# The front of a one-layer hybrid decoder kernel: how x and the first weights are loaded, where ScalarE loads its table, and how the S5 parameters share GpSimd

## The chip, the cores and the metric

The kernel runs on 1 core of one Trainium2 chip. The metric is the device time of one execution in microseconds (us), here the median of 3 runs; lower is better. A profiled execution has a span, from its first to its last instruction, and a time of its own that is a little longer than the span.

## The reference

One layer of a decoder on 256 tokens of width 2048, all in float32. The RMS norm of x feeds one combined input projection, whose columns go to three token mixers (retention, mLSTM and S5). Their outputs are joined and projected back, added to x, and a gated convolutional feed-forward layer of inner width 5632 and a last norm follow.

```python
def reference(x, norm1_w, w_in, ...):
    h = rmsnorm(x, norm1_w[l])
    x = x + token_mixer(h, w_in[l], ...)      # retention, mLSTM, S5, then @ w_out
    h = rmsnorm(x, norm2_w[l])
    x = x + conv_ffn(h, ffn_w_up[l], ffn_conv_w[l], ffn_conv_b[l], ffn_w_down[l])
    return rmsnorm(x, final_norm_w)

def s5(u, a_re, a_im, log_step, b_re, b_im, ...):
    step = jnp.exp(log_step)[:, None]
    mag = jnp.exp(ar * step)
    abar_re, abar_im = mag * jnp.cos(ai * step), mag * jnp.sin(ai * step)
    xr, xi = abar_re - 1.0, abar_im
    den = ar * ar + ai * ai
    fr, fi = (xr * ar + xi * ai) / den, (xi * ar - xr * ai) / den
    bbar_re = fr[..., None] * br - fi[..., None] * bi
    ...
```

The S5 parameters (`step`, `mag`, cosine and sine, `fr`, `fi`, and powers of the rotation) depend on weights alone. The norm's factor 1/rms depends on x; the kernel multiplies it in behind the projection.

## The kernel before, in words

Every product is made of three: a weight item is loaded as float32 (`wr`), rounded by ScalarE to a shorter type (`wh`, line 193), and the rest is taken by VectorE (`wl = wr - wh`, line 183). TensorE multiplies both by the activations (line 234). Items are cut from one long stream in the order of use and numbered from 0. There are 4 buffers for `wr`, 4 for `wh` and 3 for `wl`. `loads_to`, `highs_to` and `lows_to` issue load, rounding and rest of the items up to a number.

The front is the projection to the S5 input u: items 0 to 3 of 512 columns (one k-tile of 128 rows each) and 4 to 9 of 1024 columns (two k-tiles each). Its loop runs over these 10 items, splits the k-tiles of x that belong to one into high and low part (`s`), and adds into four accumulators (two `acc`, one `u` of double size). In its later steps it also squares x for the norm. x comes in pieces, `load_x`, on the same queue (SP) as the weights. In the loop of before, step j issues the load of the x piece and the weight item of step j+4.

Behind the front come 6 tiles of 128 output rows (two items of 1024 columns each, from item 10 on), then tiles that are token-major. The norm's factor is taken as follows: TensorE sums the squares (`mis <- onesm,s`), VectorE scales the sum (`t <- mis`), GpSimd raises it to -1/2 (`t <- t,neg_half`), VectorE puts it on a diagonal (`s <- ident,t`), and TensorE spreads it over the partitions (`mis <- s,onesm`); the last stands in TensorE's program between two matmul groups of the 6 tiles.

The order in this half of the program is written by a planner while the kernel is built: side tasks are generators that yield the engine and the time from which they can go on, and `pump` resumes one when the estimated clock of that engine (`clk.dve`, `clk.pe`, ...) has come that far. Each engine then runs its own instructions strictly in that order. `s5_params` is such a task: some 125 small GpSimd instructions of 128x12 to 128x16, issued through `Pool` (line 217) and costed by it. In the kernel before, it yields once ahead of a reciprocal on VectorE and once behind all powers of the rotation, so all that GpSimd has to do for it stands in one row.

Of the kernel before, what the change touches and what calls it, by code (L numbers as in the profile page):

```python
# [10 lines left out]
F32 = mybir.dt.float32  # L11
# [29 lines left out]
def kernel(ctx: ExitStack, tc: tile.TileContext, a: dict, out: bass.AP):  # L41
# [162 lines left out]
    class Pool:  # L204

        @staticmethod
        def __getattr__(fn):
            real = getattr(nc.gpsimd, fn)

            def go(o, *args, **kw):  # L210
                n = free(o)
                if fn == "tensor_tensor":
                    c = 0.3 + 0.1645 * n if kw["op"] == ALU.pow else 0.148 + 0.0021 * n
                else:
                    c = 0.16 + 0.00083 * n
                run("pool", c, [o], args + tuple(kw.values()))
                return real(o, *args, **kw)  # L217
            return go
# [155 lines left out]
    def loads_to(i):  # L374
        while nxt[0] <= min(i, len(items) - 1):
            j = nxt[0]
            ap, n = items[j]
            t = reuse("wr", wraw.tile([128, CH], F32, tag="wr", name=f"wr{j}"), 4)
            for i, z in enumerate(ap):
                nc.sync.dma_start(out=t[:, i * n // len(ap):(i + 1) * n // len(ap)], in_=z)  # L380
            if not auto[0]:
                free_at = max([x[3] for x in was_read.get(t.tensor.name, ())], default=0.0)
                clk.dma = max(clk.dma, free_at + 1.3) + n / 703.0
                landed(t, clk.dma + 0.91)
            if later:

                dst, src = later.pop(0)
                nc.sync.dma_start(out=dst, in_=src)
                clk.dma += free(dst) / 703.0
                landed(dst, clk.dma + 0.91)  # L390
                loaded.add(dst.tensor.name)
            raw[j] = t
            nxt[0] += 1
# [36 lines left out]
    neg_half = const.tile([128, 12], F32, name="neg_half")  # L430

# [140 lines left out]

    def s5_params():
        sh = [128, 16]
        step_ = exp_(P("ls"), sh)
        arg, th = tn(sh), tn(sh)
# [10 lines left out]
        G.tensor_scalar(ph, ph, 0.125, None, op0=MUL)  # L587
        G.tensor_tensor(z, ph, ph, op=MUL)
        G.tensor_scalar(s, z, -1 / 5040, None, op0=MUL)
        G.tensor_scalar(v, z, 1 / 40320, None, op0=MUL)  # L590
        for cs, cc in ((1 / 120, -1 / 720), (-1 / 6, 1 / 24), (None, -0.5)):
            if cs is not None:
                G.scalar_tensor_tensor(s, s, cs, z, op0=ADD, op1=MUL)
            G.scalar_tensor_tensor(v, v, cc, z, op0=ADD, op1=MUL)
        G.scalar_tensor_tensor(s, s, 1.0, ph, op0=ADD, op1=MUL)
        G.tensor_scalar(v, v, 1.0, 1.0, op0=MUL, op1=ADD)
        mag = exp_(arg, sh)

# [8 lines left out]
        for _ in range(3):  # L607
            v, s = square(v, s)
        ar, ai = P("are"), P("aim")
# [7 lines left out]
        yield after(den)  # L617
        V.reciprocal(den, den)
        for o, x0, x1_, op in ((fr, xr_, xi_, ADD), (fi, xi_, xr_, SUB)):
            G.tensor_tensor(t1, x0, ar, op=MUL)  # L620
            G.tensor_tensor(t2, x1_, ai, op=MUL)
            G.tensor_tensor(o, t1, t2, op=op)
            G.tensor_tensor(o, o, den, op=MUL)
        turn = {1: (v, s)}
        for m in (1, 2, 4, 8, 16, 32, 64):
            turn[2 * m] = square(*turn[m])
        yield after(fi)
# [486 lines left out]
    nc.gpsimd.memset(onesm, 1.0)  # L1114
    nc.gpsimd.memset(neg_half, -0.5)
    clk.dma += 0.15

    warm = mis_t()
    for _ in range(11):
        mm(warm[:, :128], lhsT=onesm, rhs=onesm, start=True, stop=True)  # L1120
    clk.pe = 5.6
# [15 lines left out]
    for j in range(4):  # L1137
# [30 lines left out]
    clk.dve = 3.3  # L1168
    clk.act = 2.8
# [10 lines left out]
    for j, ks in enumerate(kts):  # L1180
# [13 lines left out]
        if j + 4 < NU:  # L1194
            load_x(kts[j + 4][0], len(kts[j + 4]))
# [8 lines left out]
        if j >= NU - 7 and len(sqs) < 8:  # L1204
            square()
# [354 lines left out]
```

## Time and profile before

| | |
|---|---|
| median of 3 runs | 1166.82 us (1166.51 to 1167.03) |
| profiled execution, its own time | 1166.34 us |
| its span | 1164.3 us |
| TensorE busy in the span | 1141.4 us, 98% |
| VectorE, ScalarE, GpSimd busy | 868.8, 625.9, 86.3 us |
| TensorE's granted clock, mean of the span | 0.992 |

TensorE is busy almost all the time; what it loses it loses in few places. "Busy" counts an instruction as long as it lasts, so at the lower of the two clocks TensorE is busy twice as long for the same work. The profiled execution lies 0.48 us under the median of the runs.

### The profile page before, as it was taken

Reading aid. Unit: us, or ns where it says so; the run is one execution under the profiler, and the core shown is the slowest. Engines: PE = TensorE matmul, PEld = TensorE weight load, DVE = VectorE, ACT = ScalarE, POOL = GpSimd, SP = SyncE. Lnnn points to the kernel's source line nnn. Section 1 sums busy time; section 2 is a strip of 40 time slices with the busy share of each in tenths; the row PEclk is TensorE's granted clock in tenths of the full one; section 3 lists DMA queues with packets and bytes.
Section 4 is the critical chain, followed back from the end, with each engine's and each line's share of the span. In section 5 each row is a group of like instructions: output and inputs, shape, how many; then the busy total and the mean of one; then the engine's idle time right before and its main releaser. Section 6 shows DMA issues by size and latency. Waiting matters only on the chain.

```text
span 1164.3 us, 18162 instructions
## 1 busy us (share of the span) xinstructions
PE 1141.4 (98%) x6742; PEld 1015.7 (87%) x6742; DVE 868.8 (75%) x1479; ACT 625.9 (54%) x982; POOL 86.3 (7%) x226
## 2 busy tenths in 40 slices
PE   8699999999999999999999999999999999999997
PEld 7589888999988888888888888888888888888897
DVE  7488999989968668778777778777787655544554
ACT  7275546456657556555555555555555544444441
POOL 7704311001000000000000000000000000000000
PEclk9899999999999999999999999999999999999998
DMA  8546745545657656565555656555566666666663
GB/s 291 164 138 185 238 134 154 163 136 163 188 186 239 201 181 189 186 190 187 190 189 187 192 185 193 185 189 191 185 192 187 184 184 193 186 190 186 194 193 106
DMA packets 66906, 215.21 MB, mean 185 GB/s; under 512 B 7553, under 2 KB 9601, under 8 KB 66817
## 3 DMA queue, kind: packets, MB, share of 16 engines
q1 hardware_dynamic: 66672, 214.01, 59.1%
q8 instruction: 52, 0.85, 0.3%
q14 instruction: 38, 0.30, 0.1%
q10 hardware_dynamic: 144, 0.04, 0.0%
HBM read 211.92 MB, written 2.10 MB: 184 GB/s over the span
## 4 chain that ended last, share of the span: by engine, by line
PE 91%; POOL 6%; issue 1%; DVE 1%; DMA 0%; POOLq 0%; ACT 0%; DVEq 0%
PE acc L234 87%; POOL tp L217 3%; PE mis L234 3%; POOL t L217 2%; PE wo L234 1%; DVE s L183 1%; PE mis L238 0%; DVE wl L183 0%; DMA pp<-in_pp_dram 0%; DVE t L183 0%; POOLq L1556 0%; ACT s L202 0%; DVE tp L183 0%; DVEq L1556 0%; PE pj L234 0%
## 5 line engine op out<-in xcount | busy, mean ns | idle before, releaser
L183 DVE TENSOR_TENSOR wl<-wr,wh 128x1024 fp32r<-128x1024 f32 (+3 forms) x415 | 480.7, 1160 | 240.4 <-PE acc L234 211.2
L193 ACT CAST wh<-wr 128x1024 fp32r<-128x1024 f32 (+3 forms) x415 | 413.0, 997 | 372.8 <-PE acc L234 330.7
L234 PE MATMUL acc<-s,wh 128*128 128x512 f32 x2372 | 604.1, 394 | 3.3 <-DVE s L183 3.3
L234 PEld LDWEIGHTS acc<-s,wh 128*128 128x128 f32 x2372 | 426.6, 189 | 81.1 <-DVE s L183 4.2
L234 PEld LDWEIGHTS acc<-s,wl 128*128 128x128 f32 x2372 | 327.5, 190 | 26.0 <-DVE wl L183 1.0
L234 PE MATMUL acc<-s,wl 128*128 128x256 f32 x2372 | 336.6, 282 | 0.5 <-DVE wl L183 0.5
L234 PE MATMUL acc<-wh,s 128*128 128x384 f32 (+2 forms) x632 | 158.4, 329 | 0.0
L183 DVE SCALAR_TENSOR_TENSOR s<-s,pp,s 128x255 f32<-128x255 f32 (+3 forms) x244 | 116.2, 479 | 5.7 <-ACT s L202 2.6
L183 DVE TENSOR_TENSOR s<-s,s 128x256 f32<-128x256 f32 (+5 forms) x242 | 111.5, 474 | 5.5 <-ACT s L193 2.8
L234 PEld LDWEIGHTS acc<-wh,s 128*128 128x128 f32 x632 | 112.2, 189 | 1.9 <-issue 1.2
L234 PE MATMUL acc<-wl,s 128*128 128x384 f32 (+2 forms) x316 | 103.1, 326 | 0.0
L202 ACT ACTIVATE s<-s,pp 128x256 f32<-128x256 f32 (+1 forms) x146 | 82.4, 568 | 24.2 <-DVE s L183 24.1
L217 POOL TENSOR_TENSOR t<-t,neg_half 128x2 f32<-128x2 f32 (+1 forms) x4 | 2.5, 633 | 882.1 <-DVE t L183 882.1
L202 ACT ACTIVATE s<-s 128x256 f32<-128x256 f32 (+2 forms) x106 | 45.6, 431 | 33.3 <-DVE s L183 33.1
L183 DVE TENSOR_TENSOR s<-acc,s 128x256 f32<-128x256 f32 x138 | 57.4, 417 | 4.4 <-PE acc L234 3.2
L234 PEld LDWEIGHTS acc<-wl,s 128*128 128x128 f32 x316 | 59.6, 189 | 0.0
L193 ACT COPY s<-acc 128x256 f32<-128x256 f32 x136 | 49.3, 364 | 12.5 <-PE acc L234 12.5
L234 PE MATMUL acc<-g,wh 128*128 128x512 f32 x196 | 50.0, 394 | 0.0
L183 DVE TENSOR_TENSOR s<-s,rbc 128x256 f32<-128x256 f32 x106 | 44.5, 424 | 4.2 <-ACT rbc L193 1.3
L234 PEld LDWEIGHTS acc<-g,wh 128*128 128x128 f32 x196 | 34.8, 188 | 6.2
L234 PE MATMUL mis<-s,s 128*32 128x256 f32 (+6 forms) x280 | 29.4, 352 | 0.0
L234 PEld LDWEIGHTS acc<-g,wl 128*128 128x128 f32 x196 | 27.1, 189 | 2.3
(106 smaller groups left out, 467.5 us busy)
## 6 DMA issues: line engine op xcount, KB each, us to landing
wr<-in_wup_dram SPq DMA_DIRECT2D x176, 512.0 KB, 4.7
wr<-in_wdn_dram SPq DMA_DIRECT2D x70, 512.0 KB, 3.8
wr<-in_wtm_dram SPq DMA_DIRECT2D x56, 384.0 KB, 3.4
wr<-in_wfm_dram SPq DMA_DIRECT2D x36, 512.0 KB, 4.5
wr<-in_wout_dram SPq DMA_DIRECT2D x26, 512.0 KB, 4.6
wr<-in_wdt_dram SPq DMA_DIRECT2D x11, 512.0 KB, 3.8
s<-in_x_dram SPq DMA_DIRECT2D x14, 256.0 KB, 5.4
wr<-in_wdn_dram SPq DMA_DIRECT2D x14, 256.0 KB, 2.7
```

The costliest lines, as they stand in the source:

```text
L183: return real(o, *args, **kw)
L193: return nc.scalar.copy(o, i)
L202: return nc.scalar.activation(o, i, fn, **kw)
L217: return real(o, *args, **kw)
L234: nc.tensor.matmul(o, lhsT=lhsT, rhs=rhs, start=start, stop=stop)
```

## The change

Five things. All x pieces and all 10 items of the front are loaded ahead of the loop; items 4 to 9 go into six of the eight `s4` buffers, which the S5 groups use later on, in place of `wr` buffers. A small ScalarE activation of one column stands at the very start of ScalarE's program, and the table load ahead of it. The S5 task yields after each few instructions until the planner's VectorE clock reaches its GpSimd clock (`keep_up`), and the planner's cost of a small GpSimd instruction is raised to some 0.4 us. The reciprocal of `den` becomes a power of -1 on GpSimd. And 9 instead of 11 warm-up matmuls, one square fewer ahead of its time, and other start values of the planner's clocks.

```diff
-                    c = 0.3 + 0.1645 * n if kw["op"] == ALU.pow else 0.148 + 0.0021 * n
+                    c = 0.3 + 0.1645 * n if kw["op"] == ALU.pow else 0.4 + 0.0021 * n
                 else:
-                    c = 0.16 + 0.00083 * n
+                    c = 0.4 + 0.00083 * n
...
-            t = reuse("wr", wraw.tile([128, CH], F32, tag="wr", name=f"wr{j}"), 4)
+            if NS <= j < NU:
+
+                t = s4()
+            else:
+                t = reuse("wr", wraw.tile([128, CH], F32, tag="wr", name=f"wr{j}"), 4)
...
+    neg_one = const.tile([128, 16], F32, name="neg_one")
...
+    def keep_up():
+
+        return "dve", clk.pool
+
     def s5_params():
         sh = [128, 16]
         step_ = exp_(P("ls"), sh)
+        yield keep_up()
...
         mag = exp_(arg, sh)
+        yield keep_up()
...
         for _ in range(3):
             v, s = square(v, s)
+            yield keep_up()
...
-        yield after(den)
-        V.reciprocal(den, den)
+        G.tensor_tensor(den, den, neg_one, op=ALU.pow)
+        yield keep_up()
...
         for m in (1, 2, 4, 8, 16, 32, 64):
             turn[2 * m] = square(*turn[m])
-        yield after(fi)
+            yield keep_up()
...
+    nc.scalar.activation(tn([128, 1]), onesm[:, 0:1], AF.Square)
...
-    for _ in range(11):
+    for _ in range(9):
...
-    for j in range(4):
+    for j in range(NU):
         load_x(kts[j][0], len(kts[j]))
         loads_to(j)
...
-        if j + 4 < NU:
-            load_x(kts[j + 4][0], len(kts[j + 4]))
         loads_to(j + 4)
...
-        if j >= NU - 7 and len(sqs) < 8:
+        if j >= NU - 6 and len(sqs) < 8:
             square()
```

On GpSimd, the power for the norm's factor (`t <- t,neg_half`) stood behind the last power of the rotation:

```order
L217 TENSOR_TENSOR tp_660<-t_654 128x16
L217 TENSOR_SCALAR tp_664<-t_654 128x16
L217 TENSOR_TENSOR t_662<-tp_664,t_653 128x16
L217 TENSOR_SCALAR t_661<-tp_660 128x16
L217 TENSOR_TENSOR t_708<-t_597,neg_half 128x2
L664 MEMSET s_177_950 128x16
```

In the changed kernel it stands behind the second exponential (`mag`, the row `t_559`) and ahead of the first square of the rotation:

```order
L218 TENSOR_TENSOR tp_528<-tp_556,tp_527 128x16
L218 TENSOR_SCALAR tp_560<-tp_528 128x16
L218 TENSOR_TENSOR t_559<-tp_560,tp_529 128x16
L218 TENSOR_TENSOR t_632<-t_480,neg_half 128x2
L218 TENSOR_TENSOR tp_684<-t_488 128x16
L218 TENSOR_SCALAR tp_688<-t_488 128x16
```

It has moved ahead of 54 instructions of the S5 task; one more memset and the power of -1 have come in elsewhere in the row.

On VectorE, the stretch from the last sums of the front to the norm's diagonal (`s <- ident,t`) held two `wl` items with four products of the S5 matrices between them, and the reciprocal stood three rows ahead of its first row:

```order
L183 TENSOR_TENSOR s_146_678<-u_123,s_145_676 128x256
L183 TENSOR_TENSOR s_148_682<-u_123,s_147_680 128x256
L183 TENSOR_SCALAR t_597<-mis_598 128x2
L183 TENSOR_TENSOR wl_690<-wr_538,wh_570 128x1024
L183 TENSOR_TENSOR s_150_710<-s_95_441,t_274 128x512
L183 TENSOR_TENSOR s_152_712<-s_96_442,t_275 128x512
L183 TENSOR_TENSOR wl_722<-wr_561,wh_688 128x1024
L183 TENSOR_TENSOR s_151_711<-s_96_442,t_274 128x512
L183 TENSOR_TENSOR s_153_713<-s_95_441,t_275 128x512
L183 TENSOR_TENSOR s_156_744<-acc_560,s_155_742 128x256
L183 TENSOR_TENSOR wl_751<-wr_685,wh_720 128x1024
L183 TENSOR_SCALAR s_157_769<-ident,t_708 128x128 x2
```

In the changed kernel the same stretch reads (`wl_584` is item 13, `wl_666` item 16):

```order
L183 TENSOR_TENSOR s_105_573<-u_149,s_104_571 128x256
L183 TENSOR_TENSOR s_107_577<-u_149,s_106_575 128x256
L183 TENSOR_TENSOR wl_584<-wr_418,wh_450 128x1024
L183 TENSOR_TENSOR wl_613<-wr_441,wh_582 128x1024
L183 TENSOR_SCALAR t_480<-mis_602 128x2
L183 TENSOR_TENSOR s_112_636<-acc_440,s_111_634 128x256
L183 TENSOR_TENSOR wl_643<-wr_579,wh_611 128x1024
L183 TENSOR_TENSOR wl_666<-wr_608,wh_641 128x1024
L183 TENSOR_SCALAR s_118_692<-ident,t_632 128x128 x2
L183 TENSOR_TENSOR s_120_698<-acc_607,s_119_696 128x256
```

The reciprocal and the S5 products are gone from here (the products now stand some 45 rows further on, behind the `wl` of item 27), and one more item has its `wl` ahead of the diagonal: up to item 16, before up to item 15. On TensorE the spreading of the factor stands behind the five items 10 to 14, before behind the four items 10 to 13.

On the SP queue the order of the loads is the same, but the weight loads from item 4 on (`wr_293`, now `s_6_125`) waited for VectorE, which had to free a `wr` buffer:

```order
L1130 DMA s_76_291<-in_x_dram 128x512 [waits DMAHW1_49]
L380 DMA wr_293<-in_wu_dram 128x1024 [waits DMAHW2_49,DVE_49]
L1130 DMA s_78_310<-in_x_dram 128x512 [waits DMAHW3_49]
L380 DMA wr_312<-in_wu_dram 128x1024 [waits DMAHW4_49,DVE_49]
L1130 DMA s_80_329<-in_x_dram 128x512 [waits DMAHW5_49]
```

Now they wait for an earlier transfer alone:

```order
L1150 DMA s_5_123<-in_x_dram 128x512 [waits DMAHW1_49]
L385 DMA s_6_125<-in_wu_dram 128x1024 [waits DMAHW2_49]
L1150 DMA s_7_127<-in_x_dram 128x512 [waits DMAHW3_49]
L385 DMA s_8_129<-in_wu_dram 128x1024 [waits DMAHW4_49]
L1150 DMA s_9_131<-in_x_dram 128x512 [waits DMAHW5_49]
```

What has gone is the wait for VectorE; the wait for the transfer that used the same semaphore some 8 transfers earlier stays.

## Rows read from the trace of the kernel before

**Rows 1.** The page, part on the engines: busy us, share of the span, instructions

```profile
PE 1141.4 (98%) x6742; PEld 1015.7 (87%) x6742; DVE 868.8 (75%) x1479; ACT 625.9 (54%) x982; POOL 86.3 (7%) x226
```

**Rows 2.** Waits of TensorE, whole span: us in total, times, longest

```profile
PE mis L234 <- DVE s L183: 9.5, 2, 9.2
...
PE mis L238 <- POOL t L217: 1.2, 1, 1.2
```

**Rows 3.** Stretches: busy of PE, PEld, DVE, ACT, POOL; granted clock, DMA share, GB/s

```profile
9.00:10.00 1.00, 0.34 (x2) 0.30 (x3) 1.00 (x3) 1.00 (x3) 0.83 (x3) 1.00 1.14 313
14.00:15.00 1.00, 0.16 (x1) 0.16 (x2) 1.00 (x3) 1.00 (x2) 0.85 (x3) 0.99 1.05 418
15.00:16.00 1.00, 1.00 (x3) 0.81 (x4) 1.00 (x3) 1.00 (x3) 0.85 (x3) 0.50 1.01 404
18.00:19.00 1.00, 1.00 (x6) 0.81 (x5) 1.00 (x2) 1.00 (x4) 0.91 (x2) 0.80 0.99 381
55.00:56.00 1.00, 0.41 (x1) 0.41 (x2) 0.94 (x3) 0.00 (x0) 0.15 (x3) 0.50 0.00 0
59.00:60.00 1.00, 1.00 (x6) 0.82 (x6) 1.00 (x5) 1.00 (x2) 0.00 (x0) 0.82 0.00 0
```

**Rows 4.** TensorE in order of time: start, us, instruction, [idle before]

```profile
5.64 0.70 PE L234 MATMUL acc<-s,wh 128*128 128x512 f32 x2 [0.17 <-DVE s L183]
...
9.66 0.73 PE L234 MATMUL acc<-s,wh 128*128 128x512 f32 x2 [0.99 <-DVE s L183]
...
14.84 1.12 PE L234 MATMUL acc<-s,wh 128*128 128x512 f32 x2 [2.13 <-DVE s L183]
...
33.30 2.02 PE L234 MATMUL acc<-s,wh 128*128 128x512 f32 x8
...
45.14 1.21 PE L234 MATMUL acc<-s,wl 128*128 128x256 f32 x8 [0.55 <-DVE wl L183]
55.59 1.22 PE L234 MATMUL mis<-s,onesm 128*128 128x256 f32 x2 [9.24 <-DVE s L183]
```

**Rows 5.** VectorE in order of time, from 41 us on

```profile
41.82 0.25 DVE L183 RECIPROCAL t<-t 128x16 f32<-128x16 f32 x1 [6.41 <-POOL t L217]
...
55.05 0.48 DVE L183 TENSOR_SCALAR s<-ident,t 128x128 f32<-128x128 f32 x2 [4.91 <-POOL t L217]
```

**Rows 6.** GpSimd in order of time

```profile
13.33 1.13 POOL L217 TENSOR_SCALAR tp<-t 128x16 f32<-128x16 f32 x1
...
28.08 0.61 POOL L217 TENSOR_SCALAR tp<-t 128x16 f32<-128x16 f32 x1
...
37.95 0.22 POOL L217 TENSOR_TENSOR t<-tp,tp 128x16 f32<-128x16 f32 x1
...
54.29 0.73 POOL L217 TENSOR_TENSOR t<-t,neg_half 128x2 f32<-128x2 f32 x1
```

**Rows 7.** ScalarE in order of time, first 13 us

```profile
3.18 1.28 ACT L202 ACT_TABLE_LOAD   x1 [3.18 <-DMA s<-in_x_dram]
4.47 0.51 ACT L202 ACTIVATE s<-s,pp 128x256 fp32r<-128x256 f32 x1
...
12.09 1.05 ACT L193 CAST wh<-wr 128x1024 fp32r<-128x1024 f32 x1 [1.66 <-DMA wr<-in_wu_dram]
```

**Rows 8.** SP queue in order of time: issue of item 4

```profile
4.47 0.43 SPq L1130 DMA_DIRECT2D s<-in_x_dram  x1
6.24 0.33 SPq L380 DMA_DIRECT2D wr<-in_wu_dram  x1
```

**Rows 9.** The powers on GpSimd by form: busy us, mean ns

```profile
L217 POOL TENSOR_TENSOR t<-tp,neg_half 128x12 f32<-128x12 f32 x2 | 5.4, 2679 | 0.2
L217 POOL TENSOR_TENSOR t<-t,neg_half 128x2 f32<-128x2 f32 x2 | 1.4, 714 | 153.7 <-DVE t L183 153.7
```

**Rows 10.** VectorE in the front: `wl` of two steps that follow each other

```profile
15.71 1.24 DVE L183 TENSOR_TENSOR wl<-wr,wh 128x1024 fp32r<-128x1024 f32 x1
...
18.27 1.23 DVE L183 TENSOR_TENSOR wl<-wr,wh 128x1024 fp32r<-128x1024 f32 x1
```

More of the change, by code (lines that the diff above doesn't have):

```diff
@@ L608, in s5_params @@
             v, s = square(v, s)
+            yield keep_up()
         ar, ai = P("are"), P("aim")
@@ L616, in s5_params @@
         G.tensor_scalar(xr_, xr_, 1.0, -1.0, op0=MUL, op1=ADD)
-        yield after(den)
-        V.reciprocal(den, den)
+        G.tensor_tensor(den, den, neg_one, op=ALU.pow)
+        yield keep_up()
         for o, x0, x1_, op in ((fr, xr_, xi_, ADD), (fi, xi_, xr_, SUB)):
@@ L623, in s5_params @@
             G.tensor_tensor(o, o, den, op=MUL)
+            yield keep_up()
         turn = {1: (v, s)}
@@ L626, in s5_params @@
             turn[2 * m] = square(*turn[m])
-        yield after(fi)
+            yield keep_up()
         yield "obj", lambda: "raws" in st
@@ L1114 @@
     nc.gpsimd.memset(onesm, 1.0)
+    nc.scalar.activation(tn([128, 1]), onesm[:, 0:1], AF.Square)
     nc.gpsimd.memset(neg_half, -0.5)
+    nc.gpsimd.memset(neg_one, -1.0)
     clk.dma += 0.15
     warm = mis_t()
-    for _ in range(11):
+    for _ in range(9):
         mm(warm[:, :128], lhsT=onesm, rhs=onesm, start=True, stop=True)
-    clk.pe = 5.6
+    clk.pe = 4.8
     xr, xat = [None] * 8, {}
@@ L1167 @@
     ups += [pair[:, :512], pair[:, 512:]]
-    clk.dve = 3.3
-    clk.act = 2.8
+    clk.dve = clk.pool = 3.3
+    clk.act = 2.6
     sqs = []
```

## The prediction

> **What bounds the kernel now.** I read the page first: TensorE is busy 1141.4 of 1164.3 us [rows 1], so the kernel is bound by TensorE, and a change can only win what TensorE loses by waiting or by running at the lower clock. Then I read who TensorE waits for [rows 2]: one wait of 9.2 us on VectorE is far ahead of the others. Third, TensorE in order of time [rows 4] shows that nearly all that is lost lies in the first 60 us, and fourth, the clock of short stretches [rows 3] shows what each long wait costs afterwards.
>
> There are two losses. The first is in the front. TensorE starts on it at 5.64, waits 0.99 us ahead of 9.66 and 2.13 us ahead of 14.84, and is through at 33.30 [rows 4]. Right after the second wait the granted clock is 0.50 (1.2 GHz); it is back at 2.4 GHz in 18 to 19, whose mean is 0.80, so at 18.40 [rows 3]. That is 3.4 us at half speed from 14.98 on: 1.7 us lost. The remaining 12 k-tiles therefore cost (33.30 - 14.84 - 1.7) / 12 = 1.40 us each.
>
> The second is the wait for the norm's factor. The matmul that spreads it starts at 55.59 after 9.24 us of idling, and 0.55 us were lost ahead of 45.14 [rows 4]. VectorE idles 4.91 us for GpSimd ahead of the diagonal, and 6.41 us ahead of the reciprocal [rows 5]; GpSimd comes to the norm's power only at 54.29, for 0.73 us [rows 6]. So the wait is GpSimd's: the power stands behind the whole S5 task. When TensorE goes on at 55.59 the clock is 0.50, until 59.36 (mean 0.82 in 59 to 60) [rows 3]: 1.9 us more. Sum of the second loss: 9.24 + 0.55 + 1.9 = 11.7 us.
>
> **The change, part by part.** The sum is made against the profiled execution's own time, 1166.34 us, which is 0.48 us under the median of the runs.
>
> *The table load.* It takes 1.28 us from 3.18 on, behind x's first piece, and the first ACTIVATE follows at 4.47 [rows 7]. Moved ahead of the data it lies beside the transfer, and TensorE can start some 1.0 us earlier, also since two warm-up matmuls are gone. I count nothing: k-tile 2 is not there earlier, so the wait ahead of 9.66 only grows from 0.99 to about 2 us.
>
> *The loads of the front.* Item 4 was issued at 6.24, although the queue was free at 4.90 [rows 8], and landed at 12.09, where ScalarE had waited 1.66 us for it [rows 7]; from there it took 2.75 us of rounding, rest and split until 14.84 [rows 4]. Without the wait for a buffer it can be issued 1.3 us earlier. It lands 1.3 us earlier if the transfers ahead of it leave room, and not at all earlier if they do not. The transfer rate was 313 GB/s in 9 to 10 and 404 to 418 later on [rows 3], so there was some room; I take 0.9 us, keep 0 and 1.3. The later items are no issue: one step of the loop takes VectorE 18.27 - 15.71 = 2.56 us [rows 10], TensorE 2 x 1.40 = 2.80. As to the clock: the wait ahead of item 4 shrinks from 2.13 us to some 1.3, but the one ahead of 9.66 grows. After 0.99 us the clock did not fall, after 2.13 it did; I give an even chance, half of 1.7 us. Front: 0.9 + 0.8 = 1.7 us won (bounds 0 and 1.3 + 1.7 = 3.0), so its end comes at 31.6.
>
> The Trainium skill ("DMA: Bandwidth & Descriptors", section Specifications) gives some 358 GB/s as what HBM yields to one core. The rows go to 418 GB/s, so this trace does not agree. By an estimate from the page's figure the 313 of 9 to 10 would be seven eighths of what is to be had, item 4 would come 0.3 us earlier at most, and the sum below would end 0.6 us later.
>
> *The norm's power ahead of 54 S5 instructions.* When does GpSimd reach it now? Ahead of it are the same instructions up to the end of the second exponential. Before, 46 of them took from 13.33 to 38.17 [rows 6], 0.54 us each; in the stretch where VectorE was always busy, 13.33 to 28.08, the 23 took 0.64 us each. VectorE will be busier now, as it no longer idles for the reciprocal, so I take 0.64 throughout: 13.33 + 46 x 0.64 = 42.8, and 43.5 with the power. At the other rate it would be 38.9. When is it wanted? TensorE took 46.35 - 33.30 - 0.55 = 12.5 us from the front's end through four items (10 to 13) and the sum of squares, some 3.0 us an item. Now five items stand ahead: 31.6 + 15.5 = 47.1. From diagonal to matmul it is 55.59 - 55.05 = 0.54 us, so the factor is wanted by 46.6. It is there 3 us earlier (3.1 to 7.7). VectorE comes to the diagonal when item 16 has its `wl`, that is when item 13 has left its buffer at 44.1, plus 1.23 us: 45.3, in time too.
>
> So the 9.24, the 0.55 and the 1.9 us at half speed all go: 11.7 us. What is late next is the work behind the factor: some 12 products of 128x256 on VectorE, 5 us, stand ahead of the `wl` of item 18, which would be ready at about 54. TensorE wants it three items and the high half of a fourth after 47.6, at 58. That is covered by 4 us.
>
> *The reciprocal as a power.* On VectorE it took 0.25 us, and VectorE stood 6.41 us for it [rows 5]; that idling is inside the 11.7. On GpSimd the power of 128x12 takes 2.68 us and of 128x2 0.71 [rows 9], 0.197 us an element, so 128x16 is 3.5 us by my estimate (no less than 2.68). It is hidden: its result goes into the S5 products, which now stand behind the `wl` of item 27. GpSimd has 27 instructions between the two powers and that result, at 0.64 us 17.3 us, and the power's 3.5: 43.5 + 20.8 = 64.3. Item 27's `wl` waits until item 24 is through, seven items of 3 us and three of 2.2 after 47.6, some 74 us. Cover 10 us. Without cover it would cost VectorE 3.5 us and TensorE as much.
>
> *The rest.* The 1.2 us wait for the gates' GpSimd chain [rows 2] may go, since that task's place is now planned with dearer instructions; the S5 products and groups come later against TensorE and may make new small waits. I put this at 0, with -1.2 and +3 as bounds.
>
> Sum: 1.7 + 11.7 + 0 = 13.4 us; 1166.34 - 13.4 = **1152.9 us**.
>
> **The rivals.**
>
> *The factor is still late.* GpSimd runs one instruction while VectorE runs one: 13.33 took 1.13 us beside a `wl` of 1.23, where others take 0.22 [rows 6, 10]. If VectorE, now with hardly a pause, held it to about 0.9 us an instruction, the power would come at 13.33 + 46 x 0.9 + 0.7 = 55.4, TensorE would wait 9 us with the half clock behind it, and only the 1.7 us of the front and the changed place of one item (3.0 us) would remain: some 1161. Half of that delay gives 1157. Against it: no stretch of [rows 6] is slower than 0.64 over many instructions. The Trainium skill ("GPSIMD Engine Reference", section 8, Key points) says that GpSimd shares its SBUF interfaces with VectorE and contends with instructions that have two SBUF inputs. The 1.13 us agree with it, and nearly all VectorE work of the front is of that kind.
>
> *A later wait gives it back.* VectorE's S5 work is put off behind item 27, so it is denser between 70 and 360 us. If the S5 groups end late, TensorE stands ahead of the output projection, and 4 to 8 us of the win are lost, with the half clock: 1157 to 1161. Against it: VectorE idled 6.41 and 4.91 us for GpSimd alone [rows 5], 11.3 of the 13.4 us that are taken away, so it loses hardly any time in which it worked.
>
> *Slower.* Should GpSimd's power of -1 and its 27 instructions end behind 74 us, VectorE stands at the S5 products, and behind them stand the `wl` of items 28 on; three `wl` buffers are 6 us, and then TensorE stands too, at half speed afterwards. The kernel is slower once this wait is over 13.4 us and 2.3 (0.2%), that is if GpSimd comes at about 96 us instead of 64. Price then: 1169 or more. It would need over 1.8 us an instruction.
>
> *The early loads do nothing.* Item 4 lands no earlier and the clock falls as before: 1154.6. That is inside the forecast's range.
>
> **How the numbers follow.** Forecast with its bounds: win 8.5 to 15.9 us (0 and 3.0 for the front, 11.7, -3 and +1.2 for the rest, none at its worst together), chance 0.74. Factor late, 1157 to 1161: 0.11. Later wait, 1157 to 1161: 0.09. Slower: 0.03. No effect that shows, if two of these meet: 0.03. The range 1150.5 to 1158.5 takes the forecast and the milder half of the two rivals beside it, and leaves some 2 in 10 out. 0.2% (2.3 us) is about what a measurement of this kernel can tell from no change; faster by more than that 0.94, within it 0.03, slower 0.03.
>
> **What would show it right or wrong.** Right: no wait over 1 us on TensorE between the front's end and 100 us; the power of 128x2 on GpSimd at 39 to 44 us, and VectorE's diagonal waiting for TensorE's buffers and not for GpSimd; the clock at 2.4 GHz from 35 to 60 us; the front's end at 30.3 to 33.3; the power of 128x16 some 3.5 us long; no VectorE wait at the S5 products. Wrong: a wait of VectorE for GpSimd ahead of the diagonal of more than 3 us, the front's end unchanged with its waits moved ahead, or TensorE waits over 2 us in total between 100 and 430 us.

## The result and the profile after

The changed kernel takes 1158.63 us (median of 4 runs, 1158.35 to 1159.89), the kernel before 1166.66 beside it (4 runs). The ratio is 0.9936, 95% interval 0.9924 to 0.9947: 8.0 us faster, where 13.4 were forecast, and just above the forecast range. The profiled execution has 1158.52 us and a span of 1156.5 (before 1164.3).

The page, part on the engines, and TensorE's waits over the whole span, as [rows 1, 2] of before:

```profile
PE 1140.5 (99%) x6738; PEld 1013.0 (88%) x6738; DVE 870.0 (75%) x1478; ACT 625.0 (54%) x983; POOL 95.0 (8%) x228
```

```profile
PE acc L235 <- DVE s L183: 4.3, 5, 1.5
PE mis L235 <- POOL t L218: 1.9, 1, 1.9
PE mis L235 <- DVE s L183: 1.9, 4, 1.0
PE mis L239 <- DVE s L183: 1.2, 1, 1.2
...
```

The wait of 9.2 us is gone. (The 1.9 us for GpSimd's `t` is in the tail of both kernels.) Yet TensorE is busy 1140.5 us, hardly less than the 1141.4 before, although the half-speed stretches are gone too: matmuls that wait in the middle of a group count as busy. In the rows further on, 28 matmuls of the last S5 group are busy 3.29 us, where all 32 take 1.93 in the kernel before.

**The first 60 us** went as forecast. The same places as [rows 4], in TensorE's order of time:

```profile
4.85 1.20 PE L235 MATMUL acc<-s,wh 128*128 128x512 f32 x2
...
9.50 0.73 PE L235 MATMUL acc<-s,wh 128*128 128x512 f32 x2 [0.99 <-DVE s L183]
...
14.04 0.73 PE L235 MATMUL acc<-s,wh 128*128 128x512 f32 x2 [1.50 <-DVE s L183]
...
30.95 2.00 PE L235 MATMUL acc<-s,wh 128*128 128x512 f32 x8
...
45.81 0.59 PE L235 MATMUL mis<-s,onesm 128*128 128x256 f32 x2
...
49.04 2.00 PE L235 MATMUL acc<-s,wh 128*128 128x512 f32 x8
```

The front ends 2.35 us sooner (30.95, before 33.30), the factor's matmul waits for nothing, and item 16 starts at 49.04. In the kernel before, item 16 is this row:

```profile
63.46 2.00 PE L234 MATMUL acc<-s,wh 128*128 128x512 f32 x8
```

TensorE is **14.4 us ahead** here. The clock did not fall: the granted clock in stretches of [rows 3] reads 1.00 (2.4 GHz) after the second wait and behind the factor.

```profile
15.00:16.00 1.00, 1.00 (x8) 0.87 (x8) 1.00 (x2) 1.00 (x3) 0.92 (x2) 1.00 1.01 393
55.00:56.00 1.00, 1.00 (x6) 0.80 (x5) 1.00 (x1) 0.88 (x2) 1.00 (x2) 1.00 0.80 171
```

GpSimd in order of time has the norm's power at 39.85 (before 54.29, [rows 6]) and the new power of 128x16; VectorE's diagonal, second fence, follows a `wl` that waited for TensorE's buffers and does not wait for GpSimd any more [rows 5]:

```profile
39.85 0.73 POOL L218 TENSOR_TENSOR t<-t,neg_half 128x2 f32<-128x2 f32 x1
...
47.70 3.09 POOL L218 TENSOR_TENSOR t<-t,neg_one 128x16 f32<-128x16 f32 x1
```

```profile
43.28 1.23 DVE L183 TENSOR_TENSOR wl<-wr,wh 128x1024 fp32r<-128x1024 f32 x1 [1.62 <-PE acc L235]
44.42 0.48 DVE L183 TENSOR_SCALAR s<-ident,t 128x128 f32<-128x128 f32 x2
```

**From 300 to 333 us** 6.6 of the 14.4 us are given back. TensorE in order of time there:

```profile
302.50 1.87 PE L235 MATMUL acc<-s,wh 128*128 128x512 f32 x7
304.53 0.50 PE L235 MATMUL acc<-s,wh 128*128 128x512 f32 x1 [0.16 <-DVE s L183]
...
315.23 0.71 PE L235 MATMUL acc<-s,wh 128*128 128x512 f32 x2
316.56 0.50 PE L235 MATMUL acc<-s,wh 128*128 128x512 f32 x1 [0.61 <-DVE s L183]
318.08 0.50 PE L235 MATMUL acc<-s,wh 128*128 128x512 f32 x1 [1.02 <-DVE s L183]
318.42 0.65 PE L235 MATMUL acc<-s,wl 128*128 128x256 f32 x4
318.90 1.09 PE L235 MATMUL acc<-s,wh 128*128 128x512 f32 x4
319.82 0.64 PE L235 MATMUL acc<-s,wl 128*128 128x256 f32 x4
...
325.98 0.63 PE L235 MATMUL mis<-s,s 128*32 128x256 f32 x4
327.06 3.29 PE L235 MATMUL mis<-s,s 128*32 128x256 f32 x28 [0.45 <-DVE s L183]
330.28 0.96 PE L235 MATMUL mis<-s,wh 128*128 128x512 f32 x3
332.27 0.51 PE L235 MATMUL mis<-s,wh 128*128 128x512 f32 x1 [1.03 <-DVE s L183]
332.61 0.64 PE L235 MATMUL mis<-s,wl 128*128 128x256 f32 x4
```

Read it by starts, not by the numbers in brackets. Four matmuls of the output projection take from 315.23 to 318.42, 3.2 us; the next four, from 318.90, take 0.9: 2.3 us lost, on the last rests of the mLSTM heads. The last S5 group's 32 matmuls take from 325.98 to 330.28, 4.3 us, where they took 1.9 in the kernel before (first row of the fence below): 2.4 lost. The gated linear unit's first four take 2.3 instead of 0.9: 1.4 lost, on what is made of that group. With 0.5 at 302.5 to 304.9 that is 6.6 us, of which the brackets show 3.3. 14.4 - 6.6 = 7.8 us, the difference of the spans. Elsewhere the two kernels come out even: the matmul at 302.50 starts at 317.05 in the kernel before, still 14.55 us later, and the gates' 1.2 us moved from 123 to 182 us.

Why there? VectorE's S5 work, before (first fence) and after: the first products with B, the first scan, the sum that ends the last group.

```profile
45.01 1.30 DVE L183 TENSOR_TENSOR s<-s,t 128x512 f32<-128x512 f32 x2
...
126.10 0.72 DVE L183 TENSOR_TENSOR_SCAN s<-t,s 128x128 f32<-128x128 f32 x2
...
330.98 0.48 DVE L183 SCALAR_TENSOR_TENSOR s<-s,pp,mis 128x256 f32<-128x256 f32 x1 [0.90 <-PE mis L234]
```

```profile
73.25 1.28 DVE L183 TENSOR_TENSOR s<-s,t 128x512 f32<-128x512 f32 x2
...
166.50 0.73 DVE L183 TENSOR_TENSOR_SCAN s<-t,s 128x128 f32<-128x128 f32 x2
...
330.39 0.48 DVE L183 SCALAR_TENSOR_TENSOR s<-s,pp,mis 128x256 f32<-128x256 f32 x1 [1.58 <-PE mis L235]
```

S5 starts 28 us later, its scans 40 us later, and it ends nearly when it did before: 330.4 us, before 331.0. What TensorE waits for at 332.27 is the last product that is made of that sum. That product and its reader, before (two rows) and after, with the last S5 group's matmuls of before on top:

```profile
328.97 1.93 PE L234 MATMUL mis<-s,s 128*32 128x256 f32 x32
...
332.51 0.42 DVE L183 TENSOR_TENSOR s<-s,s 128x256 fp32r<-128x256 f32 x1
...
340.02 0.40 PE L234 MATMUL mis<-s,wh 128*128 128x512 f32 x1
```

```profile
331.79 0.42 DVE L183 TENSOR_TENSOR s<-s,s 128x256 fp32r<-128x256 f32 x1 [0.92 <-ACT s L193]
```

In the kernel before, the product lay ready 7.1 us (332.93 to 340.02) until TensorE came for it. In the changed kernel it is ready 0.7 us sooner, at 332.21, and TensorE already stands there and reads it at 332.27. So TensorE can keep 7.1 + 0.7 = 7.8 us of its lead, and that is what the kernel has won.

VectorE in stretches, before and after (third number after the span: VectorE busy):

```profile
0.00:60.00 60.00, 45.96 (x235) 39.49 (x236) 36.54 (x65) 31.62 (x54) 45.16 (x136) 0.89 0.66 221
60.00:120.00 60.00, 60.00 (x355) 56.62 (x355) 51.26 (x125) 36.92 (x65) 16.23 (x40) 1.00 0.57 169
120.00:300.00 180.00, 178.70 (x1144) 161.96 (x1144) 171.46 (x368) 101.23 (x171) 23.07 (x48) 1.00 0.55 162
```

```profile
0.00:60.00 60.00, 56.52 (x315) 49.79 (x316) 44.51 (x76) 43.09 (x75) 50.72 (x116) 1.00 0.75 259
60.00:120.00 60.00, 60.00 (x354) 56.45 (x353) 48.85 (x112) 34.14 (x57) 26.70 (x71) 1.00 0.67 206
120.00:300.00 180.00, 178.58 (x1126) 164.44 (x1124) 169.10 (x357) 97.24 (x163) 15.76 (x39) 1.00 0.54 158
300.00:330.00 30.00, 27.55 (x188) 20.47 (x187) 28.74 (x58) 13.61 (x21) 0.00 (x0) 1.00 0.52 173
```

VectorE works 8.0 us more in the first 60 us and 4.8 less from there to 300: at 300 us it has been busy 3.2 us more, and TensorE is 14 us further. From 300 to 330 us VectorE is full (28.74 of 30 us); from 60 to 300 it is not, it idles 22 us there (before 17).

### The profile page after: what moved, and what is told of

The parts are those of the page before. It is cut to its first block, busy times and chain, and to the rows that moved or that the text cites. A ratio compares the mean times of both kernels' runs of the same rounds, so it can differ in the third digit from the quotient of the medians.

```text
span 1156.5 us, 18142 instructions
## 1 busy us (share of the span) xinstructions
PE 1140.5 (99%) x6738; PEld 1013.0 (88%) x6738; DVE 870.0 (75%) x1478; ACT 625.0 (54%) x983; POOL 95.0 (8%) x228
## 4 chain that ended last, share of the span: by engine, by line
PE 95%; DVE 3%; issue 1%; DMA 1%; SPq 0%; ACT 0%; POOL 0%; POOLq 0%; DVEq 0%; ACTq 0%
PE acc L235 90%; PE mis L235 3%; DVE s L183 2%; DVE wl L183 1%; PE wo L235 1%; PE u L235 1%; DMA s<-in_wu_dram 1%; PE mis L239 0%; SPq L1150 0%; SPq L385 0%; POOL t L218 0%; ACT wh L193 0%; ACT s L202 0%; DVE tp L183 0%; POOLq L1574 0%
## 5 line engine op out<-in xcount | busy, mean ns | idle before, releaser
L183 DVE TENSOR_TENSOR wl<-wr,wh 128x1024 fp32r<-128x1024 f32 (+3 forms) x409 | 473.4, 1158 | 247.8 <-PE acc L235 219.8
L193 ACT CAST wh<-wr 128x1024 fp32r<-128x1024 f32 (+3 forms) x409 | 406.4, 996 | 383.6 <-PE acc L235 338.0
L183 DVE TENSOR_TENSOR s<-s,s 128x256 f32<-128x256 f32 (+4 forms) x242 | 111.2, 474 | 7.3 <-ACT s L202 3.2
```

Of the source, the lines that this page charges most:

```text
L193: return nc.scalar.copy(o, i)
```

## The experiments

All times are medians; the kernel before, run beside them, lies at 1166.2 to 1166.6. The question is what the 6.6 us are. Theory 1, called B from run 5 on, says that VectorE has too much work up to 330 us, wherever it lies. Theory 2 says that the planner put S5 work in the wrong place of the program (order); as theory A, from run 5 on, it says that the last S5 groups stand where VectorE has no time to spare. Rival C: any shift of the order brings its own waits. D: the dearer costs, which put the S5 work off, are the loss. E: VectorE is full from 120 us on, so a shift only moves the waits.

**The halves alone, and less VectorE work.** Run 1 takes S5's part out of the change, the planner's costs included (first lines of the diff), run 2 the front's part (next lines, loads in the loop again). Runs 3 and 4 leave out three of four convolution taps in the changed kernel and in the one before (last lines):

```diff
-            yield keep_up()
...
-        G.tensor_tensor(den, den, neg_one, op=ALU.pow)
+        yield after(den)
+        V.reciprocal(den, den)
```
```diff
-            if NS <= j < NU:
-                t = s4()
...
-    for j in range(NU):
+    for j in range(4):
         load_x(kts[j][0], len(kts[j]))
```
```diff
-            y = yield from conv_task(ps, 4, P("cw", 4 * i, 4 * i + 4), ...)
+            y = yield from conv_task(ps, 1, P("cw", 4 * i + 3, 4 * i + 4), ...)
```

Run 1. 

> The front's half of the change alone: all loads ahead, the early table load, 9 warm-up matmuls; the S5 task in one row and the reciprocal on VectorE as in the kernel before. Every theory says that the norm's power stays behind the whole S5 task, at some 53 to 55 us, so that TensorE, 2.4 us sooner at the factor, waits 2.4 us longer for it: front's end at 31, item 16 at 63, 1166 us (1165 to 1167). If the front were worth its 2.4 us by itself it would be 1164.

Measured 1166.92, ratio 1.0007 (0.9998 to 1.0016): as expected, the front alone wins nothing. VectorE's diagonal stands 4.72 us for GpSimd, whose power comes at 55.44.

Run 2. 

> The S5 half alone: S5 task in pieces, power in place of the reciprocal, the planner's costs; loads, table load and warm-up as before. The factor is in time, so item 16 starts at about 51.5 us instead of 49.0 in the changed kernel (63.5 before). Theory 1 (VectorE's backlog: from 60 to 330 us VectorE has more work than TensorE leaves it time for, so TensorE's lead is worth only as much as VectorE gains): VectorE's idle time of the front grows too, but part of the 2.4 us was given back at 300 to 333 us anyway, so 1159 to 1160.5. Theory 2 (order: the waits at 300 to 333 us come from where the planner has put the S5 instructions, at a price of its own): the 2.4 us are lost in full, 1161.

Measured 1161.60, 0.9955 (0.9942 to 0.9967): the front is worth 3.0 us on top of the pieces. The waits at 300 to 333 us are the same to 0.02 us, only 2 us later. Theory 2's 1161 is nearer than theory 1's 1159 to 1160.5, by too little to decide: the five executions go from 1159.1 to 1162.0.

Run 3. 

> The changed kernel, with three of the four taps of the mLSTM convolution left out: 36 VectorE instructions of 128x256 (some 0.45 us each, 16 us) between 130 and 250 us; TensorE's work stays the same. Theory 1 (VectorE's backlog): TensorE's waits at 300 to 333 us go, and all of the some 6.6 us that were given back return: 1152 us (1151 to 1153.5). Theory 2 (order): the S5 groups still stand where they stood against the output projection, 1157.5 to 1159.

Run 4. 

> The kernel before, with the same three taps left out, for comparison: there VectorE was never waited for between 124 and 429 us. Both theories: 1165.5 to 1167, the gates' wait of 1.2 us gone at most.

Measured 1159.21 (0.9940, 0.9927 to 0.9952) and 1169.87 (1.0032, 1.0019 to 1.0044). Neither expectation held, since the planner, with less to place, wrote another order; theory 2's range is missed by only 0.2 us in run 3, but its S5 groups did not stay where they stood. In run 3 the last S5 group ended at 296.8 us and 300 to 333 us cost one wait of 0.45; but at 180 us a new wait came, and the mean clock of 150 to 200 us was 0.93. GpSimd, ScalarE and TensorE of run 3:

```profile
167.40 4.36 POOL L218 TENSOR_SCALAR tp<-t 128x12 f32<-128x12 f32 x1
```

```profile
172.14 3.58 ACT L202 ACTIVATE s<-s,t,t 128x128 f32<-128x128 f32 x9 [6.10 <-POOL t L218]
```

```profile
180.37 0.56 PE L239 MATMUL mis<-ident,s 6*128 6x6 f32 x4 [4.03 <-DVE s L183]
```

ScalarE stood 6.1 us for GpSimd, 4.4 of them for one small instruction, with roundings behind it. So leaving work out lets the order change, and the next runs hold it or change it alone.

**Order held, work cut.** Run 5 shortens the taps, but the planner goes on counting their full cost; run 6 makes the last 16 products copies in the same way:

```diff
-            V.scalar_tensor_tensor(y[:, d:], t[:, :T - d], ...)
+            run("dve", 0.129 + 0.00104 * (T - d), [y[:, d:]], ...)
+            nc.vector.scalar_tensor_tensor(y[:, d:d + 16], t[:, :16], ...)
```
```diff
+                    if c >= 2:
+                        run("dve", 0.068 + 0.00104 * 512, [no[:, e]], (zo[:, e], x))
+                        nc.vector.tensor_copy(no[:, e], zo[:, e])
```

Run 5. 

> The changed kernel with the 36 convolution taps between 110 and 250 us worked on 16 columns in place of 253 to 255, everything else in the same order on every engine (some 0.3 us less VectorE work each, 11 us in all). The run with three taps left out had let the order change too: its S5 task ended 33 us sooner and its waits at 300 to 333 us were nearly gone, but a wait of 4.0 us for the gates came in at 180 us. With the order held, theory A (the place of the S5 work: the last groups stand at 262 to 330 us, where VectorE has no time to spare, and VectorE cannot run ahead of TensorE, so time won before 250 us does not carry) says that the waits at 300 to 333 us stay: 1157.0 to 1158.6 us, at most the 1.2 us wait at 182 us gone. Theory B (backlog: VectorE's whole work up to 330 us counts, wherever it is cut) says that they go: 1152 to 1154.

Run 6. 

> The changed kernel with the 16 last products of 128x512 of the last two S5 groups (between 262 and 329 us) done as copies of their first operand, same order: about half as long, 0.3 us less each, 4 to 5 us in all, three quarters of it between 290 and 329 us. Theories A and B both say that TensorE gets most of it back: 1154.5 to 1156.5 us. If the waits there come from the S5 chain's many steps (a scan after a sum after a product, each waiting for the one ahead) and not from VectorE's being full, nothing comes back: 1157.5 to 1159.

Run 5 measured 1159.54 (0.9940, 0.9927 to 0.9952). TensorE's waits are those of the changed kernel, 1 us later:

```profile
317.60 0.50 PE L235 MATMUL acc<-s,wh 128*128 128x512 f32 x1 [0.61 <-DVE s L183]
319.12 0.50 PE L235 MATMUL acc<-s,wh 128*128 128x512 f32 x1 [1.02 <-DVE s L183]
```

With the order fixed, 8.4 us less VectorE work between 120 and 300 us do not carry to 300: theory B falls. Theory A's range is missed by 0.9 us; in the execution that was traced the clock was lower in the front (a mean of 0.97 in the first 60 us, 1.00 in the changed kernel's), where nothing was edited. Run 6 measured 1157.22 (0.9923, 0.9910 to 0.9935), 1.4 us better, not separated from the changed kernel by the intervals. That is less than theories A and B expected, and nearer to the third possibility on record, that the waits come from the chain of S5 steps (1157.5 to 1159). The two waits of 1.02 us stayed. One of them is a chain indeed: ahead of the gated linear unit's product VectorE itself idles 1.58 us for TensorE and 0.92 for ScalarE, the same to 0.01 us in the changed kernel and in runs 5, 6, 8 and 11. So the last 1.4 of the 6.6 us are no sign of a full VectorE.

**Order changed, work kept.** Runs 7 to 12 are full computations: tables ahead of `fr`, `fi` and the products with B (blocks of `s5_params` in another order); the allowance `SLACK` 0.8 for 0.35; the S5 tasks ahead of the mLSTM heads (and the gates ahead of the retention heads), with the new and with the old GpSimd costs; the gated linear unit one item later; the old costs alone:

```diff
-    SLACK = 0.35
+    SLACK = 0.8
```
```diff
-    add(ret_heads())
     add(gates())
-    add(ml_heads())
+    add(ret_heads())
     add(s5_params())
...
     add(s5_gelu())
+    add(ml_heads())
```
```diff
-((4,), 0, 8), None, ((5,), 0, 8), ((4, 5), 8, 12)]
+((4,), 0, 8), ((5,), 0, 8), None, ((4, 5), 8, 12)]
```
```diff
-                    c = 0.3 + 0.1645 * n if kw["op"] == ALU.pow else 0.4 + 0.0021 * n
+                    c = 0.3 + 0.1645 * n if kw["op"] == ALU.pow else 0.148 + 0.0021 * n
...
-                    c = 0.4 + 0.00083 * n
+                    c = 0.16 + 0.00083 * n
```

Run 7. 

> The changed kernel, full computation, with one change of order inside the S5 task: the powers of the rotation and the sine and cosine tables come ahead of the reciprocal power, fr, fi and the products with B, since the tables do not need these. VectorE's first table instruction then no longer waits for GpSimd's power of -1 and the B products. Theory A (place of the S5 work): the task starts its VectorE work sooner, VectorE's idle time between 60 and 120 us (11 us) shrinks, the S5 groups end sooner and the waits at 300 to 333 us shrink with them: 1153 to 1156.5 us. Rival C (the planner's other tasks move too, and waits of the same size come in elsewhere, as the gates' wait did): 1157.5 to 1160.

Run 8. 

> The changed kernel, full computation, with the planner's allowance for side tasks ahead of TensorE raised from 0.35 to 0.8 us, so that VectorE takes S5 work sooner. Theory A: less VectorE idle time before 300 us, smaller waits at 300 to 333 us, some new waits for the rests of items: 1154 to 1158 us. Rival C (order decides, any shift of it brings its own waits): 1158 to 1162.

Run 9. 

> The changed kernel, full computation, with the S5 tasks ahead of the mLSTM heads in the planner's list (gates, retention heads, S5, mLSTM heads). In the program the end of the last S5 group on VectorE (its sum with D u) then stands behind the rest of item 112, in the changed kernel behind that of item 119 and in the kernel before behind 116; the last rests of the mLSTM heads stay where they are, behind 112 to 116. Theory A (the loss at 300 to 333 us is the place of the S5 work against TensorE's stream): the 3.6 us that TensorE loses on the last group (its matmuls from 326 us on and the wait ahead of the gated linear unit at 332) go, the 2.3 us at 315 to 318, ahead of the last mLSTM rests, may stay: 1154 to 1156.5 us. Rival C (any shift brings waits of the same size elsewhere): 1158 to 1161.

Run 10. 

> As the run with the S5 tasks ahead of the mLSTM heads, and with the planner's old, lower costs of GpSimd instructions besides: the first table instruction stands behind item 23's rest instead of 32's, the last S5 group's end behind 112 as there. Theory A: as that run, 1154 to 1156.5 us, with more of VectorE's idle time before 100 us used, if the GpSimd results are there in time; if they are not, VectorE waits for GpSimd at the first products and tables, TensorE behind it, and it is 1158 or more.

Run 11. 

> The changed kernel, full computation, with the gated linear unit one item of the output projection later (after the first two thirds of tile 5 in place of before). Theory A: 2.8 us of TensorE work then stand between the last S5 group and the wait for it, so 2 to 2.8 us of the 3.6 us go, and the unit's own outcome, with 2.8 us of cover left of 5.6, costs up to 1 us: 1156 to 1157.5 us. If the loss were a matter of VectorE's being full there, the wait moves and stays: 1158.5.

Run 12. 

> The changed kernel, full computation, with the planner's old, lower costs of GpSimd instructions. The first table instruction stands behind the rest of item 23 (21 in the kernel before, 32 in the changed one), the last S5 group's end behind 119 as in the changed kernel. Theory A: the last group's place decides, and it has not moved, so about the same loss at 300 to 333 us: 1157.5 to 1160 us. Rival D (the dearer costs, which put off the start of the S5 work by ten items, are what gave the win back): the loss goes, 1153 to 1155.

Measured 1163.98, 1160.23, 1187.57, 1188.10, 1161.96 and 1168.25: all above the changed kernel, run 8 (0.9947, 0.9934 to 0.9961) not by more than the intervals. Theory A's gains came in none of the six; rival C's range held in run 8 and was too low in runs 7 and 9. In run 9 the S5 groups do end 19 us sooner, at 311, but the mLSTM heads, now behind them in the planner's list, end late, and TensorE stands 10.4 us at once for VectorE:

```profile
335.28 0.45 PE L239 MATMUL mis<-ident,s 128*128 128x128 f32 x1 [10.38 <-DVE s L183]
```

In run 11 the last S5 products moved back along with the unit (its end from 330.4 to 333.5): the wait moved and stayed. Run 12 shows what part of the change makes the factor early. With S5 in pieces and the power of -1, but the old costs, the norm's power comes at 52.56 again, and TensorE waits longer than before [rows 4]:

```profile
53.84 1.22 PE L235 MATMUL mis<-s,onesm 128*128 128x256 f32 x2 [13.11 <-DVE s L183]
```

With the pieces there, it is the dearer costs that move it, not the pieces by themselves; the dearer costs without the pieces were not run.

**The last runs.** Run 13 is run 3 with ScalarE's head norm put later; runs 14 and 15 double the last 16 products in both kernels; run 16 takes the reciprocal back alone; runs 17 and 18 raise `SLACK` to 3.0 and 4.0.

```diff
-        yield after(nb)
+        yield "dve", after(nb)[1] + (6.0 if extra is None else 0.0)
```
```diff
+                    if c > 1:
+                        nc.vector.tensor_tensor(no[:, e], zo[:, e], x, op=MUL)
```
```diff
-        G.tensor_tensor(den, den, neg_one, op=ALU.pow)
+        yield after(den)
+        V.reciprocal(den, den)
```

Run 13. 

> The changed kernel with three of the four convolution taps left out, as in the third run, and the ScalarE part of the retention head norm put 6 us later by the planner. In the third run the S5 task ended 33 us sooner and the waits at 300 to 333 us went, but ScalarE stood 6.1 us for GpSimd's head norm instructions (one of them took 4.36 us) with the rounding of two items behind it, so that TensorE waited 4.0 us at 180 us and ran at the lower clock afterwards. Theory A (place of the S5 work against TensorE's stream): with that wait gone too, 1152 to 1154.5 us. Rival C (any shift brings waits of the same size elsewhere): 1157 to 1160.

Run 14. 

> The changed kernel with the 16 last products of 128x512 of the last two S5 groups done twice, same order: 16 x 0.6 = 9.8 us more VectorE work between 262 and 329 us. Theory A (VectorE has no time to spare in that stage): most of it comes through, 1163 to 1168 us. If only the chain of the S5 steps counted and VectorE had time to spare: 1158.5 to 1161.

Run 15. 

> The kernel before with the same 16 products done twice. There TensorE waited for nothing between 124 and 429 us and VectorE idled 8 us between 300 and 340. Theory A: little comes through, 1166 to 1170 us, at least 3 us less than the same work costs in the changed kernel. If VectorE were as full there, the loss is the same in both.

Run 16. 

> The changed kernel with the reciprocal back on VectorE, all else as it is. The prediction put this part at nothing: 1157.5 to 1160 us, with VectorE's wait for GpSimd ahead of the reciprocal under 1 us. If the power is what keeps VectorE from standing for GpSimd, that wait is 3 us or more, TensorE stands behind it, and it is 1161 or more.

Run 13 measured 1154.80 (0.9901, 0.9888 to 0.9915): with S5's end at 291 us and 0.5 us of waits from 300 to 333, 3.8 us of the 6.6 are back, with less work as well as another order. Theory A's range ended at 1154.5; other waits, 1.4 us at 187, take some. Runs 14 and 15 measured 1172.99 and 1174.18: 9.8 us more work cost 14.4 us in the changed kernel and 8.0 in the one before, though TensorE never waited there for more than 0.11 us between 124 and 429 us. Part of the 14.4 is the clock: its mean from 300 to 350 us is 0.86 in run 14, 1.00 in the changed kernel. So VectorE has little time to spare in either, and theory A's guess that the kernel before would swallow it falls. The doubled products are themselves steps of the S5 chain, but in run 15 TensorE waits 0.92 us at 287 and 1.15 us at 311 for rests of items, which are not.

Run 16 measured 1170.05 (1.0029, 1.0020 to 1.0038): 11.4 us slower by one instruction. Nobody waits for it; VectorE has it at once, and the B products start at 73.32, as in the changed kernel:

```profile
56.49 0.25 DVE L183 RECIPROCAL t<-t 128x16 f32<-128x16 f32 x1
```

But the order behind it is another, and TensorE waits 2.3 us at 201 and 7.8 us between 315 and 342.

Run 17. 

> The changed kernel, full computation, with the planner's allowance for side tasks raised from 0.35 to 3.0 us. In the program the last S5 group's first products stand behind the rest of item 104 (116 in the changed kernel, 108 before), its end behind 114 (119, 116), the last mLSTM rests behind 114 to 115 (116). Theory A (place of the S5 work against TensorE's stream): the 6.7 us given back at 300 to 333 us shrink to 2 or less, small new waits for rests of items before, some 1 to 2 us: 1153 to 1156.5 us. Theory E (VectorE is full from 120 us on, so that work put sooner only moves the waits): TensorE waits for rests of items between 120 and 300 us instead, 1158 to 1163.

Run 18. 

> The same with an allowance of 4.0 us: the last S5 group's first products behind item 93, its end behind 103, the last mLSTM rests behind 110 to 114. Theory A: no loss on the S5 groups at all, but VectorE's side work may now stand 4 us ahead of an item's rest, with two items (5 us) in hand, so some waits for rests: 1152 to 1157 us. Theory E: waits for rests of items all over, 1160 or more.

Measured 1157.12 (0.9920, 0.9907 to 0.9934) and 1163.20 (0.9966, 0.9954 to 0.9978): run 17 lies between theory A's range and E's, run 18 in E's. Run 17 is the fastest full computation, but its interval overlaps that of the changed kernel. At 300 to 333 us TensorE waits for nothing; it waits 2.1 us at 160 and 1.7 for rests of items at 263 to 286 instead:

```profile
160.06 0.41 PE L239 MATMUL mis<-ident,s 6*128 6x6 f32 x4 [2.09 <-DVE s L183]
...
285.79 0.44 PE L235 MATMUL acc<-wl,s 128*128 128x384 f32 x1 [0.64 <-DVE wl L183]
```

I read this as A and E at once: the place decides where TensorE waits, VectorE's work decides that it waits. The table sets the place in the program (how many items have their rest ahead of the last S5 group's last products from TensorE's results, `s <- pj,s`, in VectorE's program) against TensorE's idle time from 290 to 350 us, added up from its waits. Runs 5, 6, 14 and 15 keep the order of the kernel that they edit and are left out:

```
kernel               place   idle 290 to 350   median
run 18 (SLACK 4)       93          1.6          1163.2
run 4 (fewer taps)     94          1.2          1169.9
run 3 (fewer taps)     99          0.9          1159.2
run 13 (fewer taps)    99          0.5          1154.8
run 17 (SLACK 3)      104          0.7          1157.1
run 10 (mLSTM last)   105         14.3          1188.1
before                108          0.0          1166.7
run 1 (front alone)   111          0.9          1166.9
run 12 (old costs)    111          1.1          1168.3
run 9 (mLSTM last)    112         20.6          1187.6
changed               116          3.5          1158.6
run 2 (pieces alone)  116          3.6          1161.6
run 11 (unit later)   116          5.0          1162.0
run 8 (SLACK 0.8)     116          5.1          1160.2
run 7 (tables first)  118          7.3          1164.0
run 16 (reciprocal)   118          7.8          1170.1
```

With the mLSTM heads where they were, the idle time is at most 1.6 us up to place 111 and 3.5 to 7.8 us from 116 on. Runs 9 and 10, with the mLSTM heads last in the planner's list, do not fit: 20.6 and 14.3 us at places 112 and 105, half of it or more in the one wait for the heads shown above. I read from it that the last dependent work counts, of whichever task it is. The median follows the idle time only where nothing else waits (run 12 stands 13.1 us for the factor, run 18 for rests of items).

## Why the prediction failed, point by point

- **Front, 1.7 us (0 to 3.0).** Right in its terms: 2.35 us in the trace, and 3.0 by run 2. Item 4 starts 0.80 us earlier (forecast 0.9), and the clock did not fall, which gave the other 1.55 (forecast an even chance of 1.7). That the chance came up is luck: runs 5 and 6 have the same front, and in their traces the clock fell. The wait ahead of k-tile 2, forecast to grow to some 2 us, stayed 0.99. No run tells the early loads from the table load and the warm-up. Item 4's load was no longer what was late: ScalarE's rounding came at 11.24 (before 12.09, [rows 7]) and waited for TensorE to free a `wh` buffer:

```profile
11.24 1.05 ACT L193 CAST wh<-s 128x1024 fp32r<-128x1024 f32 x1 [1.48 <-PE u L235]
```

- **The norm's factor, 11.7 us.** Right: 14.4 - 2.35 = 12.1 us. The power came at 39.85, near the earlier of the two times worked out (38.9; the sum took 42.8), as 46 instructions took 0.56 us each and not 0.64, and GpSimd was in time by more than was claimed.
- **Reciprocal as a power, 0.** Right as a resource (3.09 us for 3.5, nobody waits for it), wrong as an edit: undone alone it costs 11.4 us (run 16), through the order that the planner then writes.
- **The rest, 0 (-1.2 to +3).** This is the step that failed: the term for S5 work that comes later against TensorE, put at nothing. It cost 6.6 us at 300 to 333 us, twice the upper bound, because TensorE came 14 us sooner to products that were ready only 0.7 us sooner and had 7.1 us of cover. The orders of runs 7, 8, 11 and 16 put it 1.6 to 11.4 us higher still. The gates' 1.2 us did not go either; they moved. (The bounds add up to a win of 8.7 to 15.9 us; the recorded 8.5 is a slip that moves nothing.)
- **The rival "a later wait gives it back"** is what happened, at the place and time that it named (the output projection, 1157 to 1161), but at the full clock. It had 0.09. The argument against it was that 11.3 of the 13.4 us were VectorE idling for GpSimd, so that VectorE lost no working time. That confuses an idle span taken away with work done: TensorE moved 14 us forward in its program, while VectorE filled 8.0 us of its idling in the first 60 us, lost 4.8 again by 300 us (why, no run isolates; S5 work that was put off is the likely part), and was there 3.2 us further. A lead of TensorE is worth what its helpers' last outcome gains, and the cover that it had.
- **The range** ended inside that rival's span (1157 to 1161), 0.13 us under the measured time. The sign that would show the forecast wrong, TensorE waits over 2 us between 100 and 430 us, came true: 5.0 us.

Shown: the place and size of the loss, that VectorE has little time to spare there (28.74 of 30 us, runs 14, 15), that the order moves it (runs 9, 11, 16, 17). Not shown: how the 6.6 us divide between a full VectorE and the chain of S5 steps, of which at least the last 1.4 are chain. Open: whether a full computation can keep more than 9.2 us of the 14.4; none here did.

## What to carry over

When the bound engine loses a long wait early, ask of its helpers not whether they idled in that wait but whether they will be as far ahead at the next meeting point: add up the helper's busy time from the change to there in both programs, and read from the trace how long its last outcome lay ready before it was wanted. That cover, 7.1 us here, was most of the 7.8 us that TensorE could keep. Where a planner writes the order, an edit's own price can be nothing and its effect through the order over ten microseconds (run 16); compare the places of the last dependent work in the two orders, and put that into the range. Idle time in brackets showed half of this loss, 3.3 of 6.6 us; compare starts of equal groups.

## What the runs showed of the hardware

- A GpSimd instruction of 128x12, mostly 0.2 to 0.3 us, took 4.36 us in run 3, 5.36 in run 13 (from 187.93) and 10.02 in run 17:

```profile
85.47 10.02 POOL L218 TENSOR_SCALAR t<-t 128x12 f32<-128x12 f32 x1 [20.47 <-DVE t L183]
```

In run 17 VectorE worked without a pause from 85.30 to 95.38 us, and the instruction ended at 95.49. A busy VectorE alone does not make it so: in the front of the kernel before, beside one, 23 instructions took 0.64 us each. The Trainium skill ("GPSIMD Engine Reference", section 8, Key points) has GpSimd share its SBUF interfaces with VectorE; that fits, but no run here isolates the cause.
- The granted clock after the front's second wait is not told by that wait's length: 2.13 us in the kernel before was followed by 0.50 [rows 3], the same 2.13 us in run 3 by 1.00 throughout 10 to 20 us, and 1.98 us in run 5 by a mean of 0.83 there (0.50 from 15 to 17 us).
